# Block 0's stores of the second third on one queue, more weight sums on GpSimd, and planned gaps between transposed loads

## The chip, the cores and the metric

The kernel runs on one core of one Trainium2 chip. The metric is the device time of one execution in microseconds (us), the median of several runs. The engines are called PE (TensorE, matmuls), DVE (VectorE), ACT (ScalarE), POOL (GpSimd) and SP (SyncE, which here only issues DMAs).

## The reference

```python
batch, m, k, h, n = 16, 512, 768, 3072, 768     # x, w1, b1, w2: float32
y = np.matmul(x, w1) + b1
y = np.maximum(y, 0)
return np.matmul(y, w2).astype(np.float32)
```

As one matrix x has 8192 rows: 8192x768 times 768x3072, bias and ReLU, times 3072x768.

## The kernel before

**Data and tiling.** Everything is computed in fp16 with fp32 sums. The 8192 rows are 8 blocks of 1024. The 3072 columns of the first matmul are three "thirds" g = 0, 1, 2. Of a third, w1 is 8 raw pieces (2 halves of k times 4 column groups h, a "strip" being one (g, h)); of a block, x is 8 raw pieces. Instead of 32 block products the kernel makes 26, each of a sum of x pieces with a sum of w1 pieces (the tables `X_SUMS` and `W1_SUMS`: 19 and 18 additions of a 128x768 tile); the results are combined by ACT and DVE on their way out of PSUM (`add_first`; the operations are "sum", "seed", which writes into a PSUM bank that a later product adds to, and "out", which writes y). Block 0 is the exception: its first two thirds are made by plain products without sums (`first_block`, `plain`, line 1040), since the sums aren't ready yet; its last third, g = 2, is the first to use them (line 1142). Then come block 1 with g = 0, 1, 2, block 2, and so on. y goes to DRAM (`yd`) and is read back for the second matmul, which is done in the same manner (`add_second`, line 1337, with `Y_SUMS` and `W2_SUMS`).

**Names.** `v` is SBUF for the weights: `v[:, g, slot]`, 24 slots for each third. Slots 8 to 23 of `v[:, 1]` are borrowed at the start: the evictions of block 0's plain products (ACT, line 1054) write y there, 16 slots in all, for g = 0 and again for g = 1. `add_store_y` (line 1021) stores a slot to `yd`. Later the w1 sums of g = 1 (line 829) are written to the same slots, and so wait for those stores. `z` holds x pieces and their sums, `s` and `yo` results on their way, `ps` is PSUM with 8 banks.

**x of later blocks.** POOL loads rows of x with a cast to fp16 (`load_x`, line 728), and SP turns them with a transposing DMA from SBUF to SBUF (`add_turn`, line 790): eight loads and eight turns for each block. The x sums of the next block (line 815) need the turns.

**Queues.** SP's and ACT's DMAs share eight semaphores, DMAHW0 to DMAHW7, which are used in turn in the program's order. A DMA first waits until the one that had its semaphore before, eight places back, has landed; that is the first DMAHW name in its row below. POOL's DMAs have eight of their own (DMASW). [...]

**The order.** A planner (`Graph`) holds every step as a task with a cost, a queue and keys that it reads and writes; `run` simulates the engines and so settles the order of instructions of every engine, which bank and which slot each step takes; `emit` then writes the program in that order. Its costs and arrival times are numbers in the code; `preset` tells it when something is there. Tables say which engine makes a sum: `W1_POOL` and `W2_POOL` list the sums (third, number) that POOL makes instead of DVE, `X1_POOL` those of block 1's x. `OUT_ACT` says which of block 0's stores ACT issues. Changing one table therefore moves other instructions too.

## Time and profile before

| what | value |
|---|---|
| median of 3 runs | 851.57 us (851.34 to 853.14) |
| the profiled execution's own time | 852.25 us |
| its span in the trace | 850.6 us |
| PE busy | 835.0 us, 98% |
| DVE / ACT / POOL busy | 702.1 / 559.9 / 272.3 us |
| granted PE clock, mean | 0.995 |

The trace counts time from the span's start; 1.65 us of the profiled execution lie outside its span. A timeline row gives start, duration, engine, line, operation and tiles; "q" after an engine's name is its sequencer, which issues DMAs; "xN" means that N like instructions were merged, and the bracket behind gives the engine's idle time before the row and what ended it. The name in the bracket is inferred: where a wait was for several things, it is the last one that the profile saw.

### The profile page before, as it was taken

The page shows a single profiled execution, that of the slowest core. Times are in us where ns is not written, and L with a number is a line of the kernel's source. Part 1 is how long each engine was busy: PE and PEld are TensorE (multiplying, and loading weights), DVE is VectorE, ACT ScalarE, POOL GpSimd, SP SyncE. Part 2 cuts the span into 40 slices and gives each one's busy share as a digit, 9 for nine tenths or more (in the row PEclk, how much of TensorE's full clock was granted, in tenths as well). Part 3 has the DMA queues.
Part 4 walks back from the last instruction along what each step waited for, and adds up shares of the span by engine and source line. Part 5 has one row for each costly group of instructions (what it writes and reads, how often), then busy time and mean ns, then how long its engine had stood idle before and what let it go on. Part 6 is the DMA issues. An engine that isn't in the chain of part 4 may idle for free. (4 is left out here: it accounts for less than half of the span.)

```text
span 850.6 us, 17854 instructions
## 1 busy us (share of the span) xinstructions
PE 835.0 (98%) x6263; PEld 614.1 (72%) x6263; DVE 702.1 (83%) x1320; ACT 559.9 (66%) x1252; POOL 272.3 (32%) x421
## 2 busy tenths in 40 slices
PE   8969999999999999999999999999999999999998
PEld 7628888888888888888876666666656665565664
DVE  5858989798998979889999988788777788777773
ACT  4528878887888778878964555565545468757421
POOL 6445874554655446444413100011000011101000
PEclk9989999999999999999999999999999999999999
DMA  9994999999999989998888989888879899988622
GB/s 218 228 224 109 232 209 237 220 213 241 214 228 215 242 215 244 228 274 275 282 257 203 273 251 284 261 220 230 240 216 275 267 226 229 242 222 272 221 76 76
DMA packets 169168, 193.32 MB, mean 227 GB/s; under 512 B 58556, under 2 KB 144644, under 8 KB 169076
## 3 DMA queue, kind: packets, MB, share of 16 engines
q1 hardware_dynamic: 112480, 119.21, 46.2%
q0 software_dynamic: 54976, 71.00, 42.9%
q10 hardware_dynamic: 1620, 1.95, 0.7%
q8 instruction: 49, 0.80, 0.4%
q14 instruction: 43, 0.35, 0.1%
HBM read 140.39 MB, written 83.95 MB: 264 GB/s over the span
## 5 line engine op out<-in xcount | busy, mean ns | idle before, releaser
L1337 PE MATMUL ps<-v,z 128*128 128x384 f16 x2496 | 407.0, 326 | 0.9 <-ACT ps L1354 0.8
L1142 PE MATMUL ps<-z,v 128*128 128x256 f16 x3432 | 375.0, 273 | 0.0
L1142 PEld LDWEIGHTS <-v 128*128 128x128 f16 x3432 | 335.6, 98 | 39.8 <-issue 0.7
L1337 PEld LDWEIGHTS <-z 128*128 128x128 f16 x2496 | 244.0, 98 | 163.2 <-issue 2.2
L1295 DVE TENSOR_TENSOR z<-z 128x768 f16<-128x768 f16 x448 | 232.9, 553 | 42.9 <-PE ps L1337 27.7
L1021 POOL DMA_DIRECT2D yd<-z x228 | 123.7, 545 | 137.5 <-ACT z L1165 65.1
L1176 DVE CUSTOM_DVE_ANT_0 z<-ps,s 128x512 f16<-128x512 f32 x220 | 145.0, 684 | 25.9 <-PE ps L1142 15.5
L1170 ACT ACTIVATE s<-ps,bt 128x256 f32<-128x256 f32 x352 | 145.1, 473 | 14.9 <-PE ps L1142 8.3
L1354 ACT ACTIVATE s<-ps 128x384 f32<-128x384 f32 (+1 forms) x151 | 73.5, 486 | 122.2 <-PE ps L1337 115.9
L1179 DVE TENSOR_TENSOR s<-ps,s 128x512 f32<-128x512 f32 x132 | 89.5, 684 | 4.9 <-PE ps L1142 4.3
L922 POOL DMA_DIRECT2D z<-in_x_dram x32 | 22.9, 736 | 193.7 <-ACT junk L926 188.5
L815 DVE TENSOR_TENSOR z<-z 128x768 f16<-128x768 f16 x147 | 80.5, 580 | 4.3 <-PE ps L1142 4.1
L926 ACT ACTIVATE junk<-z 128x768 f16<-128x768 f16 x94 | 78.8, 838 | 0.9
L1354 ACT ACTIVATE ps<-ps 128x384 f32<-128x384 f32 x80 | 38.0, 475 | 61.6 <-PE ps L1337 60.9
L1358 DVE TENSOR_TENSOR s<-ps,s 128x384 f32<-128x384 f32 x107 | 59.2, 553 | 13.0 <-PE ps L1337 12.6
L1170 ACT ACTIVATE ps<-ps,bt 128x256 f32<-128x256 f32 x88 | 39.4, 448 | 26.2 <-PE ps L1142 17.0
L1170 ACT ACTIVATE z<-ps,bt 128x256 f16<-128x256 f32 x132 | 54.7, 489 | 2.3 <-PE ps L1142 2.3
L1179 DVE TENSOR_TENSOR ps<-ps,s 128x512 f32<-128x512 f32 x66 | 45.4, 696 | 10.7 <-PE ps L1142 6.2
L1040 PE MATMUL ps<-z,v 128*128 128x256 f16 (+1 forms) x264 | 44.9, 332 | 8.0 <-ACT v L1054 6.4
L1358 DVE TENSOR_TENSOR s<-s,ps 128x384 f32<-128x384 f32 x62 | 34.2, 552 | 21.6 <-PE ps L1337 21.2
L1165 ACT ACTIVATE s<-ps 128x512 f32<-128x512 f32 x66 | 39.8, 602 | 9.8 <-DVE z L1176 6.5
L1165 ACT ACTIVATE z<-ps 128x512 f16<-128x512 f32 x66 | 39.2, 594 | 10.6 <-DVE z L1176 5.0
(59 smaller groups left out, 340.2 us busy)
## 6 DMA issues: line engine op xcount, KB each, us to landing
z<-yd SPq DMA_DIRECT2D x128, 384.0 KB, 6.9
yd<-z POOLq DMA_DIRECT2D x228, 128.0 KB, 3.7
out_dram<-s SPq DMA_DIRECT2D x127, 192.0 KB, 6.2
yd<-z SPq DMA_DIRECT2D x124, 128.0 KB, 3.2
z<-in_x_dram POOLq DMA_DIRECT2D x34, 384.0 KB, 7.7
z<-in_x_dram POOLq DMA_DIRECT2D x56, 192.0 KB, 6.1
v<-w2d SPq DMA_DIRECT2D x36, 192.0 KB, 4.0
w2d<-in_w_dram POOLq DMA_DIRECT2D x24, 192.0 KB, 5.4
```

The source lines that it names most:

```text
L815: (self.nc.gpsimd if e == "POOL" else self.nc.vector).tensor_tensor(out=self.z[:, a], in0=self.z[:, c], in1=self.z[:, d], op=ALU.add if si ...
L926: self.nc.scalar.activation(out=self.junk, in_=src, func=ACTF.Square, accum_out=None if at is None else self.stat[:, at:at + 1])
L1021: {"POOL": self.nc.gpsimd, "SP": self.nc.sync, "ACT": self.nc.scalar}[e].dma_start(out=self.ydram[:, b, slot, g].rearrange("p s m -> p (s ...
L1142: nc.tensor.matmul(pairs(self.ps[:, at, :])[:, :, j], lhsT=self.v[:, g, w, k * self.QM + j * P:k * self.QM + (j + 1) * P], rhs=x.rearrange ...
L1165: nc.scalar.activation(out=out, in_=ps, scale=float(a), func=func if kind == "out" else ACTF.Copy)
L1170: nc.scalar.activation(out=pairs(out)[:, :, j], in_=pairs(ps)[:, :, j], func=func, scale=float(a), bias=self.bt[:, n, g, j:j + 1])
L1176: nc.vector._custom_dve(TENSOR_ADD_SAT, out=out, in0=ps, in1=s, s0=F_MAX, s1=0.0)
L1179: nc.vector.tensor_tensor(out=out, in0=in0, in1=in1, op=ALU.add if a == c else ALU.subtract)
L1295: self.nc.vector.tensor_tensor(out=self.y_view(a), in0=self.y_view(c), in1=self.y_view(d), op=ALU.add if sign > 0 else ALU.subtract)
L1337: nc.tensor.matmul(self.ps[:, bank[ch].at[0], 0:NH], lhsT=self.y_view(ys[SECOND_U[p]])[:, h // 2, h % 2 * P:(h % 2 + 1) * P], rhs=self.v[: ...
L1354: nc.scalar.activation(out=out, in_=ps, func=ACTF.Copy, scale=float(a))
L1358: nc.vector.tensor_tensor(out=out, in0=in0, in1=in1, op=ALU.add if a == c else ALU.subtract)
```

## The change

1. `OUT_ACT` is never true: block 0's eight stores of g = 1, h = 2 and 3, which ACT issued, are issued by SP.
2. `W1_POOL` has 17 sums instead of 12. `X1_POOL` stays as it is: five x sums of block 1.
3. `W2_POOL` has one more sum, (0, 17), and two neighbours of `T0_ORDER`, the order of the first group of products of the second matmul, change places.
4. The planner is told, by eight presets read by block 1's turns alone, that turn s may be planned from 44 + 0.5 s on. No instruction and no wait comes of these presets; they only shape the plan.

```diff
-W1_POOL = ((0, 14), (0, 18), (0, 20), (1, 8), (1, 10), (1, 13), (1, 16), (1, 20), (1, 23), (1, 24), (1, 25), (2, 14))
+W1_POOL = ((0, 9), (0, 10), (0, 11), (0, 13), (0, 21), (1, 8), (1, 9), (1, 12), (1, 14), (1, 20), (1, 21), (1, 23), (1, 24), (1, 25), (2, 12), (2, 14), (2, 19))
...
-OUT_ACT = lambda g, h, m, r: g == 1 and h > 1
+OUT_ACT = lambda g, h, m, r: False
...
-W2_POOL = ((0, 11), (0, 12), (0, 18), ...
+W2_POOL = ((0, 11), (0, 12), (0, 17), (0, 18), ...
...
+TURN_AT = 44, 0.5
-T0_ORDER = (13, 4, 17, 15, 12, 8, 2, 1, 10, 21, 18, 3, 25, 0, 19, 11, 23, 14, 16, 22, 7, 24, 6, 5, 20, 9)
+T0_ORDER = (13, 4, 17, 15, 12, 8, 2, 1, 10, 21, 18, 3, 25, 0, 19, 23, 11, 14, 16, 22, 7, 24, 6, 5, 20, 9)
...
         g.preset("b1_rows", 6.0)
+        for s in range(8):
+            g.preset(("turn", s), TURN_AT[0] + TURN_AT[1] * s)
...
-            reads=self.x_keys(a), writes=[("z", raw[s // 2 * 2 + k], s % 2) for k in range(2)])
+            reads=self.x_keys(a) + ([("turn", s)] if b == 1 else []), writes=[("z", raw[s // 2 * 2 + k], s % 2) for k in range(2)])
```

Since three lines are added, line 790 of before is 793 of the change, 815 is 818, 829 is 832, 1021 is 1024, 1054 is 1057, 1176 is 1179 and 1179 is 1182.

ACT at the end of block 0's second third, before: stores (line 1021) stand between the evictions of the plain products (line 1054), and the third of them waits for DMAHW6.

```order
L1054 ACTIVATE v<-ps,b1y 128x2x2x128 [waits DMAHW2_49,DMAHW1_49,PE_49]
L1054 ACTIVATE v<-ps,b1y 128x2x2x128 [waits PE_49]
L1021 DMA yd<-v 128x512 [waits DMAHW0_49,Activation_49]
L1021 DMA yd<-v 128x512 [waits DMAHW2_49]
L1054 ACTIVATE v<-ps,b1y 128x2x2x128 [waits DMAHW1_49,PE_49]
L1054 ACTIVATE v<-ps,b1y 128x2x2x128 [waits PE_49]
L1021 DMA yd<-v 128x512 [waits DMAHW6_49,Activation_49]
L1021 DMA yd<-v 128x512 [waits DMAHW0_49]
L1054 ACTIVATE v<-ps,b1y 128x2x2x128 [waits DMAHW4_49,DMAHW3_49,PE_49]
```

With the change no store is left there; the evictions wait for PE and for the stores that emptied their slots of g = 0.

```order
L1057 ACTIVATE v<-ps,b1y 128x2x2x128 [waits DMAHW2_49,DMAHW1_49,PE_49]
L1057 ACTIVATE v<-ps,b1y 128x2x2x128 [waits PE_49]
L1057 ACTIVATE v<-ps,b1y 128x2x2x128 [waits DMAHW1_49,DMAHW2_49,PE_49,Activation_49]
L1057 ACTIVATE v<-ps,b1y 128x2x2x128 [waits PE_49,Activation_49]
L1057 ACTIVATE v<-ps,b1y 128x2x2x128 [waits DMAHW4_49,DMAHW3_49,PE_49]
```

SP at the same place, before: the last store of `v` that SP makes, then block 1's eight turns (line 790) in one row; the second of them has DMAHW6.

```order
L1021 DMA yd<-v 128x512 [waits DMAHW4_49]
L790 DMA_TRANSPOSE z<-z 128x6x128 [waits DMAHW5_49,DMASW0_49,PE_49]
L790 DMA_TRANSPOSE z<-z 128x6x128 [waits DMAHW6_49,DMASW1_49]
L790 DMA_TRANSPOSE z<-z 128x6x128 [waits DMAHW7_49,DMASW2_49,PE_49]
L790 DMA_TRANSPOSE z<-z 128x6x128 [waits DMAHW1_49,DMASW3_49]
L790 DMA_TRANSPOSE z<-z 128x6x128 [waits DMAHW3_49,DMASW4_49,PE_49]
L790 DMA_TRANSPOSE z<-z 128x6x128 [waits DMAHW4_49,DMASW6_49,DMASW5_49]
L790 DMA_TRANSPOSE z<-z 128x6x128 [waits DMAHW5_49,DMASW6_49,PE_49]
L790 DMA_TRANSPOSE z<-z 128x6x128 [waits DMAHW7_49,DMASW7_49]
```

With the change four of the eight moved stores stand between the turns and four behind them.

```order
L793 DMA_TRANSPOSE z<-z 128x6x128 [waits DMAHW7_49,DMASW2_49,PE_49]
L1024 DMA yd<-v 128x512 [waits DMAHW0_49,Activation_49]
L793 DMA_TRANSPOSE z<-z 128x6x128 [waits DMAHW1_49,DMASW3_49]
L793 DMA_TRANSPOSE z<-z 128x6x128 [waits DMAHW2_49,DMASW4_49,PE_49]
L1024 DMA yd<-v 128x512 [waits DMAHW3_49,Activation_49]
L793 DMA_TRANSPOSE z<-z 128x6x128 [waits DMAHW4_49,DMASW6_49,DMASW5_49]
L1024 DMA yd<-v 128x512 [waits DMAHW5_49]
L793 DMA_TRANSPOSE z<-z 128x6x128 [waits DMAHW6_49,DMASW6_49,PE_49]
L1024 DMA yd<-v 128x512 [waits DMAHW7_49]
L793 DMA_TRANSPOSE z<-z 128x6x128 [waits DMAHW0_49,DMASW7_49]
L1024 DMA yd<-v 128x512 [waits DMAHW1_49,Activation_49]
```

POOL from the last loads of w1 (line 715) to its first store of a sum-made y, before: three w1 sums, seven loads of x, one sum, the last load of x, four sums.

```order
L715 DMA v<-in_w_dram 128x6x256 x8
L829 TENSOR_TENSOR v<-v 128x768 x3
L728 DMA z<-in_x_dram 128x768 x7
L829 TENSOR_TENSOR v<-v 128x768
L728 DMA z<-in_x_dram 128x768
L829 TENSOR_TENSOR v<-v 128x768 x4
L1021 DMA yd<-z 128x512 x2
```

With the change five sums stand ahead of the loads of x, and six in a row and one more behind the last of them.

```order
L716 DMA v<-in_w_dram 128x6x256 x8
L832 TENSOR_TENSOR v<-v 128x768 x5
L729 DMA z<-in_x_dram 128x768 x6
L832 TENSOR_TENSOR v<-v 128x768
L729 DMA z<-in_x_dram 128x768 x2
L832 TENSOR_TENSOR v<-v 128x768 x6
L1024 DMA yd<-z 128x512
L832 TENSOR_TENSOR v<-v 128x768
L1024 DMA yd<-z 128x512
```

DVE from its last 15 x sums of block 0 to the first seeds (line 1179, `ps<-ps,s`) of third g = 2, before: all its w1 sums for that third stand ahead of the first operation on its results (line 1176, shown as ISA).

```order
L815 TENSOR_TENSOR z<-z 128x768 x15
L829 TENSOR_TENSOR v<-v 128x768 x25
L1176 ISA z<-ps,s 128x512
L815 TENSOR_TENSOR z<-z 128x768
L1176 ISA z<-ps,s 128x512 x2
L1179 TENSOR_TENSOR s<-ps,s 128x512
L829 TENSOR_TENSOR v<-v 128x768 x2
L1179 TENSOR_TENSOR ps<-ps,s 128x512 x2
```

With the change 20 of them stand ahead, and five (the last of g = 2) between those operations.

```order
L818 TENSOR_TENSOR z<-z 128x768 x12
L832 TENSOR_TENSOR v<-v 128x768 x20
L1179 ISA z<-ps,s 128x512
L832 TENSOR_TENSOR v<-v 128x768 x4
L1179 ISA z<-ps,s 128x512 x2
L1182 TENSOR_TENSOR s<-ps,s 128x512
L832 TENSOR_TENSOR v<-v 128x768
L818 TENSOR_TENSOR z<-z 128x768
L1182 TENSOR_TENSOR ps<-ps,s 128x512 x2
```

## The prediction

> **What bounds the kernel now.** I read the page first, then PE's waits, then PE's timeline where the waits lie, then the engines that those waits name.

> ```profile
> span 850.6 us, 17854 instructions
> ...
> PE 835.0 (98%) x6263; PEld 614.1 (72%) x6263; DVE 702.1 (83%) x1320; ACT 559.9 (66%) x1252; POOL 272.3 (32%) x421
> ...
> PE   8969999999999999999999999999999999999998
> ...
> L1040 PE MATMUL ps<-z,v 128*128 128x256 f16 (+1 forms) x264 | 44.9, 332 | 8.0 <-ACT v L1054 6.4
> ```

> PE is busy for 98% of the span, so the change can win only where PE stands idle or runs slowly. The one hollow in its 40 slices that is not the very start is the third, from 42.5 to 63.8 us, with a 6. The plain products' group (line 1040) has 8.0 us of idle time. PE's list of waits and its timeline put that time in two places:

> ```profile
> PE ps L1040 <- ACT v L1054: 6.4, 1, 6.4
> PE ps L1040 <- DMA z<-in_x_dram: 1.5, 1, 1.5
> ...
> PE ps L1337 <- ACT ps L1354: 0.8, 1, 0.8
> ```

> ```profile
> 49.57 2.75 PE L1040 MATMUL ps<-z,v 128*128 128x512 f16 x12 [1.54 <-DMA z<-in_x_dram]
> 58.74 5.24 PE L1040 MATMUL ps<-z,v 128*128 128x512 f16 x12 [6.42 <-ACT v L1054]
> 63.81 26.37 PE L1142 MATMUL ps<-z,v 128*128 128x256 f16 x240
> ```

> Both idle stretches fall into the last products of block 0's second third. The second 12 matmuls are like the first 12 and take 5.24 us instead of 2.75. The windows tell why, by the clock in the column before the last two:

> ```profile
> 53.40:57.00 3.60, 0.00 (x0) 0.00 (x0) 1.31 (x3) 0.00 (x0) 1.12 (x1) 1.00 1.35 183
> 57.00:63.80 6.80, 5.06 (x12) 1.78 (x12) 0.00 (x0) 1.95 (x3) 2.10 (x2) 0.50 1.01 220
> 63.80:80.85 17.05, 17.05 (x158) 15.26 (x157) 13.22 (x23) 13.92 (x33) 8.41 (x10) 1.00 0.47 98
> ```

> After the long idle the granted clock is 0.50 until the first products of g = 2 begin, which costs 5.24 - 2.75 = 2.49 us more. From 63.80 on PE is busy without a gap: 26 products in 17.05 us, 0.656 each.

> What ACT does meanwhile:

> ```profile
> 46.20 2.53 ACTq L1021 DMA_DIRECT2D yd<-v  x2
> 48.83 1.26 ACT L1054 ACTIVATE v<-ps,b1y 128x512 f16<-128x512 f32 x2 [2.66 <-DMA yd<-v]
> 56.86 1.02 ACTq L1021 DMA_DIRECT2D yd<-v  x2
> 58.01 1.26 ACT L1054 ACTIVATE v<-ps,b1y 128x512 f16<-128x512 f32 x2 [7.91 <-issue]
> ```

> Its evictions, which empty the PSUM banks, stand behind its own stores. The first pair of stores holds its sequencer from 46.20 to 48.73, and the evictions begin at 48.83; of two in 1.26 us the first ends near 49.5, and PE goes on at 49.57. So I put the 1.54 to ACT too, though the row names a load of x. The second pair is issued only at 56.86; the evictions follow at 58.01, and PE goes on at 58.74. Why it is issued so late stands on SP:

> ```profile
> 46.40 15.08 SPq L790 DMA_TRANSPOSE z<-z  x8
> ```

> ```profile
> L790 SPq DMA_TRANSPOSE z<-z x3: 1362/2189/4249, 46.4 to 52.2; - x3
> ...
>   ACT v L1054: 7.9, 1
> ...
> DMA to landing us min/median/max: 5.2/8.9/9.7
> ```

> ```profile
> L790 SPq DMA_TRANSPOSE z<-z x4: 1226/1232/1307, 56.2 to 60.2; - x4
> ...
> DMA to landing us min/median/max: 2.8/3.4/4.2
> ```

> ACT's third store has DMAHW6, which the second turn had before it. The first three turns (first answer) need up to 9.7 us to land, and the answer lists ACT's line 1054 as held up 7.9 us by them. Later turns (second answer) take 1.23 us to issue and 2.8 to 4.2 to land.

> **The change, part by part.**

> *ACT's eight stores go to SP.* Nothing but evictions is left on ACT there. The evictions of 1.26 / 2 = 0.63 us are half of what 6 matmuls take (2.75 / 2 = 1.38), so ACT keeps up. I take out 1.54 + 6.42 + 2.49 = 10.45 us: the first product of g = 2 begins at 63.81 - 10.45 = 53.36. If some of the 2.49 remained (a clock that falls for another reason), the gain would be 7.96 at least.

> *The same stores on SP.* Four of the eight now stand between the turns. A store's issue on SP is

> ```profile
> L1021 SPq DMA_DIRECT2D yd<-v x24: 319/380/957, 12.7 to 44.0; - x24
> ```

> so 4 x 0.38 = 1.5 us. The last of the eight turns was issued at about 60.2; now at 61.7, and it lands 2.8 to 4.2 later, at 64.5 to 65.9. What needs it is DVE's x sum at 75.09 (below), which was 75.09 - 63.81 = 11.28 after the first product of g = 2 and would now be wanted at 53.36 + 11.28 = 64.64, plus whatever PE loses before. That is just met with the stall of the next part, missed by 1.3 at worst without it. I take nothing, and keep the miss for a rival. The other four stores stand behind the last turn; what waits for the slots that they empty are w1 sums of g = 1, wanted only a third (17.05) later. Of POOL's sums the one that needs a moved store is its sixth behind the loads, (1, 14); while it waits, POOL leaves DVE alone.

> *Five more w1 sums on POOL, fewer on DVE; DVE's last five of g = 2 now stand between operations on results.* The rows that price this are

> ```profile
> L829 DVE TENSOR_TENSOR v<-v x25: 545/552/4035, 34.5 to 54.2; 128x768 f16<-128x768 f16 x25
> L829 POOL TENSOR_TENSOR v<-v x8: 1632/1648/1952, 22.9 to 57.5; 128x768 f16<-128x768 f16 x8
> ```

> ```profile
> 34.49 3.49 DVE L829 TENSOR_TENSOR v<-v 128x768 f16<-128x768 f16 x7
> ...
> 42.12 12.60 DVE L829 TENSOR_TENSOR v<-v 128x768 f16<-128x768 f16 x15 [1.12 <-DMA v<-in_w_dram]
> 66.09 0.69 DVE L1176 CUSTOM_DVE_ANT_0 z<-ps,s 128x512 f16<-128x512 f32 x1 [11.37 <-PE ps L1142]
> ...
> 71.44 1.35 DVE L1179 TENSOR_TENSOR ps<-ps,s 128x512 f32<-128x512 f32 x2
> ...
> 73.30 0.68 DVE L1176 CUSTOM_DVE_ANT_0 z<-ps,s 128x512 f16<-128x512 f32 x1
> ...
> 75.09 0.55 DVE L815 TENSOR_TENSOR z<-z 128x768 f16<-128x768 f16 x1
> ```

> ```profile
> 46.12 3.24 POOL L829 TENSOR_TENSOR v<-v 128x768 f16<-128x768 f16 x2
> 55.88 3.23 POOL L829 TENSOR_TENSOR v<-v 128x768 f16<-128x768 f16 x2 [6.53 <-DMA yd<-v]
> 73.24 1.64 POOL L815 TENSOR_TENSOR z<-z 128x768 f16<-128x768 f16 x1 [2.46 <-PE ps L1142]
> ```

> Alone, a sum costs DVE 3.49 / 7 = 0.50 us; its slowest took 4.035, about 0.5 plus the 3.24 of the two POOL sums at 46.12. So sums of the two engines shut each other out, DVE losing. But a DVE operation on PSUM took its usual 0.68 at 73.30, wholly beside POOL's 1.64 at 73.24. [...]

> Before, DVE had finished its sums at 54.72 and waited 11.37 us for PE. That cover goes with the 10.45. The first seed (71.44) must be there when PE has made 13 products of g = 2, by the order: at 53.36 + 13 x 0.656 = 61.89. On DVE, from the end of the last x load on POOL (about 46.1, where POOL's row of sums begins), I count 11 sums at 0.50 and 5 operations on results at 0.65 up to and with that seed, and 7 POOL sums at 1.65 beside them. If nothing overlaps: 46.1 + 5.5 + 3.3 + 11.5 = 66.4, a stall of 4.5. If the operations on results run beside POOL: 63.1, a stall of 1.2. If POOL's (1, 14) and the one behind it come late enough, they fall out (3.3 less) and there is no stall. I take 1.6, near the middle value, because the row at 73.30 shows that overlap; bounds 0 and 4.5. What is late next is that seed, PE waiting on DVE at about 62.

> *Presets on the turns* make no instruction: 0 by themselves. *One y-side sum on POOL, two products swapped* (second matmul): PE's only idle time there is the 0.8 in the list of waits, at

> ```profile
> 440.00:460.00 20.00, 19.40 (x119) 11.60 (x119) 19.90 (x42) 7.29 (x15) 3.26 (x4) 1.00 0.79 229
> ```

> DVE is full there (19.90 of 20), POOL nearly empty; one sum moved may remove the 0.8 or add as much. I take 0, bounds ±0.8.

> *The rest of the run.* From 63.81 on PE has no gap to gain from. DVE is full over a long stretch without holding PE up:

> ```profile
> 70.00:100.00 30.00, 30.00 (x277) 26.86 (x276) 29.44 (x52) 24.28 (x58) 23.67 (x32) 1.00 0.85 173
> ```

> Five w1 sums fewer leave it 2.5 us more room; I take 0.

> **The sum.** The profiled execution took 852.25 us, 850.6 of it the span, and is 0.68 above the median. 852.25 - 10.45 + 1.6 = 843.4 for it; on the median 851.57 - 8.85 = 842.7.

> **The rivals.**

> *Case A*, the sum: 842.7, its own range 840.3 (no stall, and the 0.8 gone) to 844.5.

> *Case B*, DVE is shut out by POOL: nothing overlaps, the seed comes 4.5 late, and so long an idle stretch halves the clock again as the 6.42 did (2.49): 851.57 - 10.45 + 4.5 + 2.49 = 848.1; without the halving 845.6. The 4.035 speaks for it, the 0.68 at 73.30 against. From the rows, the idle time that halves the clock lies between 1.54 and 6.42. [...]

> *Case C*, the turns come late: behind stores, three more of them are slow like the median of the first three (2.19 instead of 1.23). The last turn then lands 2.9 later, up to 68.8, and PE waits for block 1's x sum by about 2.9: 845.6. For it: turns issued while loads of x still flow took up to 4.25. Against it: the four from 56.2 on did not.

> *Case D*, the stores were not what held the evictions: the 7.91 carries the name "issue", and the 1.54 that of a load. If the 6.42 and the slow clock stay, 851.57 - 1.54 = 850.0, no change that could be told. Against it: ACT's second pair of stores is issued at 56.86, and the evictions start right behind it.

> *Case E*, slower: the queue that held up ACT now holds up the turns. From 46.40 the last turn is SP's 12th DMA, and can go only when the fourth has landed. The fourth, if issued at 56.2 as the fourth turn was before, and both with landings of 9.7: 56.2 + 2 x 9.7 = 75.6, and the x sum wanted at 64.64 is 11.0 late, with 2.49 for the clock: 851.57 - 10.45 + 11.0 + 2.49 = 854.6. It decides where the last turn lands after 64.64 + 10.45 - 2.49 = 72.6. Against it: from 56.2 on the landings took 2.8 to 4.2.

> **How the numbers follow.** A 0.62, B 0.20, C 0.10, D 0.05, E 0.03. A measurement of this kernel can tell about 0.2%, 1.7 us. A, B and C are faster by more: 0.92; D is the same, 0.05; E slower, 0.03. The time is A's. The range begins at 840.6, a little above A's best, and reaches to 848.2, which holds B and C; D, E and the far ends of A, B and C, less than 0.2 together, lie outside.

> **What would show it.** PE's waits lose the 6.4 and the 1.5 at the plain products; ACT's timeline has evictions 1.3 apart up to about 54 and no store; line 1142 (then 1145) begins at 53 to 54, and the clock is 1.00 around it. A wait of PE of 1 to 2 us named after DVE's line 1182 near 62 shows A, over 4 with a clock of 0.50 behind it B; one at 64 to 69 that goes back to line 818 and a turn shows C. The prediction is wrong if PE's wait before 53 is still there, or if PE waits at a place after 70 where nothing waited before.

## The result, and the profile after

| kernel | median us (lowest to highest) | ratio to before (95% interval) |
|---|---|---|
| before, runs of the same job | 851.76 (851.31 to 853.14) | 1 |
| the change | 845.86 (844.26 to 847.78) | 0.9925 (0.991 to 0.994) |

The change is 5.9 us faster, in the direction and inside the range that were forecast, but 3.2 above the 842.7 taken as likeliest. The profiled execution took 844.51 us, 1.35 below the median. The changed kernel varies by 3.5 us from execution to execution, where before varied by 1.8 in this job; in the later jobs before varied by 1.8 to 5.3, so a wider spread of the change is not shown by these figures. All medians here are over every execution; one of the repeated change (2275 us) and one of the last kernel below (869 us) were slow, and the ratios leave these two out. The page of the profile:

```profile
span 842.7 us, 17860 instructions
...
PE   8999999999999999999999999999999999999998
...
L1043 PE MATMUL ps<-z,v 128*128 128x256 f16 (+1 forms) x264 | 42.1, 321 | 0.0
```

The 6 in the third slice is gone, and the plain products have no idle time left (8.0 before). PE's waits and the timelines of PE and ACT:

```profile
PE ps L1145 <- DVE ps L1182: 2.4, 1, 2.4
...
PE ps L1340 <- ACT ps L1357: 1.1, 2, 0.8
```

```profile
22.26 30.68 PE L1043 MATMUL ps<-z,v 128*128 128x256 f16 x174
52.78 8.68 PE L1145 MATMUL ps<-z,v 128*128 128x256 f16 x78
63.83 76.40 PE L1145 MATMUL ps<-z,v 128*128 128x256 f16 x692 [2.37 <-DVE ps L1182]
```

```profile
50.39 0.69 ACT L1057 ACTIVATE v<-ps,b1y 128x512 f16<-128x512 f32 x1 [0.61 <-PE ps L1043]
51.73 0.69 ACT L1057 ACTIVATE v<-ps,b1y 128x512 f16<-128x512 f32 x1 [0.66 <-PE ps L1043]
```

The plain products run through, ACT evicts every 1.3 us and waits for PE (one row, at 49.09, names a store instead, for 0.55), and g = 2 begins at 52.78 instead of 63.81. Then PE stands for 2.37 us, for a seed by DVE, at the place that the forecast named. DVE and POOL there:

```profile
55.05 0.69 DVE L1179 CUSTOM_DVE_ANT_0 z<-ps,s 128x512 f16<-128x512 f32 x1 [1.33 <-PE ps L1145]
...
58.87 0.68 DVE L1182 TENSOR_TENSOR s<-ps,s 128x512 f32<-128x512 f32 x1
59.47 1.51 DVE L832 TENSOR_TENSOR v<-v 128x768 f16<-128x768 f16 x1
60.90 2.26 DVE L818 TENSOR_TENSOR z<-z 128x768 f16<-128x768 f16 x1
63.09 1.28 DVE L1182 TENSOR_TENSOR ps<-ps,s 128x512 f32<-128x512 f32 x2
...
68.15 0.56 DVE L818 TENSOR_TENSOR z<-z 128x768 f16<-128x768 f16 x1 [1.39 <-DMA z<-z]
```

```profile
46.23 8.99 POOL L832 TENSOR_TENSOR v<-v 128x768 f16<-128x768 f16 x5
58.92 1.64 POOL L832 TENSOR_TENSOR v<-v 128x768 f16<-128x768 f16 x1 [3.71 <-ACT ps L1168]
...
61.09 1.65 POOL L832 TENSOR_TENSOR v<-v 128x768 f16<-128x768 f16 x1
```

The seed at 63.09 stands behind two DVE sums of 1.51 and 2.26 us, where a sum alone took 0.50 in before (3.49 / 7 at 34.49); both overlap a POOL sum, (1, 14) at 58.92 and (1, 20) at 61.09. 1.51 + 2.26 - 2 x 0.5 = 2.8, about PE's whole wait. A smaller loss follows: DVE's x sum at 68.15 waited 1.39 for a turned load, the eighth turn:

```profile
L793 SPq DMA_TRANSPOSE z<-z x2: 1251/1258/1264, 61.2 to 63.2; - x2
...
  DVE z L818: 1.4, 1
...
DMA to landing us min/median/max: 2.8/3.9/4.9
```

### The profile page after: what moved, and what is told of

It is laid out like the page before. It is cut to its first block, busy times and chain, and to the rows that moved or that the text cites. A ratio compares the mean times of both kernels' runs of the same rounds, so it can differ in the third digit from the quotient of the medians.

```text
span 842.7 us, 17860 instructions
## 1 busy us (share of the span) xinstructions
PE 832.9 (99%) x6263; PEld 613.9 (73%) x6263; DVE 702.7 (83%) x1314; ACT 560.1 (66%) x1252; POOL 282.6 (34%) x427
## 4 chain that ended last, share of the span: by engine, by line
PE 90%; DMA 0%; ACT 0%; DVE 0%; issue 0%; ACTq 0%
PE ps L1340 48%; PE ps L1145 42%; DMA z<-yd 0%; DVE z L1179 0%; ACT ps L1357 0%; ACT junk L929 0%; ACT s L1357 0%; DVE s L1182 0%; DVE s L1354 0%; PE ps L1452 0%; PE ps L1463 0%; ACTq L1357 0%
## 5 line engine op out<-in xcount | busy, mean ns | idle before, releaser
L1145 PEld LDWEIGHTS <-v 128*128 128x128 f16 x3432 | 335.8, 98 | 42.5 <-issue 3.5
L1298 DVE TENSOR_TENSOR z<-z 128x768 f16<-128x768 f16 x448 | 233.3, 553 | 43.1 <-PE ps L1340 27.2
L1179 DVE CUSTOM_DVE_ANT_0 z<-ps,s 128x512 f16<-128x512 f32 x220 | 144.7, 683 | 16.1 <-ACT ps L1173 7.9
L818 DVE TENSOR_TENSOR z<-z 128x768 f16<-128x768 f16 x147 | 85.0, 610 | 4.8 <-PE ps L1145 2.9
L925 POOL DMA_DIRECT2D z<-in_x_dram x32 | 22.9, 738 | 193.6 <-ACT junk L929 188.4
L1168 ACT ACTIVATE z<-ps 128x512 f16<-128x512 f32 x66 | 39.2, 595 | 10.7 <-PE ps L1145 5.7
L1043 PE MATMUL ps<-z,v 128*128 128x256 f16 (+1 forms) x264 | 42.1, 321 | 0.0
```

Source lines behind the costliest of these rows:

```text
L818: (self.nc.gpsimd if e == "POOL" else self.nc.vector).tensor_tensor(out=self.z[:, a], in0=self.z[:, c], in1=self.z[:, d], op=ALU.add if si ...
L1145: nc.tensor.matmul(pairs(self.ps[:, at, :])[:, :, j], lhsT=self.v[:, g, w, k * self.QM + j * P:k * self.QM + (j + 1) * P], rhs=x.rearrange ...
L1168: nc.scalar.activation(out=out, in_=ps, scale=float(a), func=func if kind == "out" else ACTF.Copy)
L1179: nc.vector._custom_dve(TENSOR_ADD_SAT, out=out, in0=ps, in1=s, s0=F_MAX, s1=0.0)
L1298: self.nc.vector.tensor_tensor(out=self.y_view(a), in0=self.y_view(c), in1=self.y_view(d), op=ALU.add if sign > 0 else ALU.subtract)
```

## The experiments

Each ran in five rounds beside the kernel before; "ratio" is to that, with its 95% interval.

| kernel | median us | ratio |
|---|---|---|
| before, only the stores to SP | 845.13 | 0.9920 (0.9899 to 0.9941) |
| the change, repeated | 845.39 | 0.9912 (0.9888 to 0.9937) |
| the change, stores back on ACT | 853.48 | 1.0020 (1.0009 to 1.0031) |
| the change, W1_POOL of before | 848.81 | 0.9954 (0.9941 to 0.9968) |
| the change, no presets | 843.77; repeated 844.54 | 0.9897 (0.9882 to 0.9912); 0.9927 (0.9914 to 0.9941) |
| the change, x sum 10 behind two seeds | 846.30 | 0.9929 (0.9908 to 0.9950) |
| the change, two POOL sums shortened | 843.40 | 0.9907 (0.9882 to 0.9933) |
| the change, (0, 9) and (1, 20) off POOL | 844.75 | 0.9911 (0.9897 to 0.9924) |
| that, turns ahead of stores | 845.16 | 0.9915 (0.9894 to 0.9936) |
| no presets, turns ahead of stores | 843.12 | 0.9888 (0.9869 to 0.9908) |
| that, (1, 12) off POOL | 845.12 | 0.9918 (0.9903 to 0.9933) |

**The stores alone.** In the kernel before:

```diff
-OUT_ACT = lambda g, h, m, r: g == 1 and h > 1
+OUT_ACT = lambda g, h, m, r: False
```

> The kernel before with ACT's eight stores given to SP, and nothing else of the change. Theory S: this alone removes PE's waits of 1.5 and 6.4 us and the slow clock, 10.5 to 10.8 us; DVE then keeps 28 sums ahead of the first seed instead of 25 of w1 with POOL's five fewer, and PE waits 0 to 3 for it: 841.5 to 845, all or more than all that the whole change brought. Rival: the other tables carry a part of the gain (POOL's five more sums spare DVE, the planned gaps keep the turns apart), so that this alone gives 846 to 850, with a longer wait for DVE near 62 or for a turn.

Measured 845.13, a ratio of 0.9920 beside the whole change's 0.9912 in the same job; the waits are in PE's timeline:

```profile
52.56 8.68 PE L1142 MATMUL ps<-z,v 128*128 128x256 f16 x78
63.08 5.40 PE L1142 MATMUL ps<-z,v 128*128 128x256 f16 x48 [1.84 <-DVE ps L1179]
69.63 5.58 PE L1142 MATMUL ps<-z,v 128*128 128x256 f16 x46 [1.15 <-DVE ps L1179]
```

One table entry carries all that the change brought, as far as these intervals can tell; the 845.13 lies 0.1 above the span that was expected. The other parts do not add up to a gain that can be told.

**The rest without the stores.** The change with the old `OUT_ACT`:

```diff
-OUT_ACT = lambda g, h, m, r: False
+OUT_ACT = lambda g, h, m, r: g == 1 and h > 1
```

> The changed kernel with the eight stores given back to ACT; all else as in the change. If the stores on ACT are what made PE wait: the waits of 1.5 and 6.4 us at the plain products come back (in sum 6 to 8) with two halved windows of the clock, and line 1145 begins near 60 to 64: 849 to 852.5. Rival: the other tables had removed the wait too (the planned gaps let an earlier turn land, so ACT's third store waits less): 845 to 847.

Measured 853.48, above the span expected and 1.6 above before. PE's timeline has both waits back, and a third, the seed's:

```profile
48.98 2.75 PE L1043 MATMUL ps<-z,v 128*128 128x512 f16 x12 [1.32 <-DMA z<-in_x_dram]
59.16 4.60 PE L1043 MATMUL ps<-z,v 128*128 128x512 f16 x12 [7.43 <-ACT v L1057]
...
73.39 1.80 PE L1145 MATMUL ps<-z,v 128*128 128x256 f16 x15 [1.11 <-DVE ps L1182]
```

So the 1.5 of before, which its row put to a load of x, was ACT's: with the stores it comes (here and before), without them it goes (in every other kernel here). It isn't the load.

**The old list of POOL's sums.**

```diff
-W1_POOL = ((0, 9), (0, 10), (0, 11), (0, 13), (0, 21), (1, 8), (1, 9), (1, 12), (1, 14), (1, 20), ...
+W1_POOL = ((0, 14), (0, 18), (0, 20), (1, 8), (1, 10), (1, 13), (1, 16), (1, 20), (1, 23), ...
```

> The changed kernel with the W1_POOL of before (12 sums on POOL instead of 17); the stores, the planned gaps and the second matmul as in the change. If the five more sums spare DVE work that PE waits for: PE's wait near 62 is 1 us or more longer than in the changed kernel, 846 to 848. If they cost DVE more than they spare it (1.65 against 0.5 each): the wait is gone or under 1, 842 to 843.5. If it hangs only on which sums happen to lie around 59 to 63: within 1 of the changed kernel, and the profile names the one or two DVE sums that stood beside a POOL sum there.

Measured 848.81, above what the first case expected. PE's wait is 4.78, two stretches of 3.41 us with a clock of 0.50 follow it (65.19 to 72.01; the first is shown), and DVE's timeline has a reason that no case named:

```profile
65.19:68.60 3.41, 2.54 (x13) 1.75 (x13) 3.20 (x6) 1.04 (x3) 1.02 (x1) 0.50 0.42 143
```

```profile
58.16 1.15 DVE L832 TENSOR_TENSOR v<-v 128x768 f16<-128x768 f16 x2 [2.60 <-DMA yd<-v]
60.45 0.78 DVE L832 TENSOR_TENSOR v<-v 128x768 f16<-128x768 f16 x1 [1.14 <-DMA yd<-v]
...
65.32 1.28 DVE L1182 TENSOR_TENSOR ps<-ps,s 128x512 f32<-128x512 f32 x2
```

DVE itself stands 2.60 and 1.14 us for the moved stores, whose slots its sums of g = 1 are to fill, and the seed comes at 65.32. In the change it is POOL's queue that stands for them:

```profile
L832 POOLq EVENT_SEMAPHORE x2: 43/5235/10427, 47.9 to 48.0; - x2
```

That wait of POOL's sequencer (line 832, after) ended at 48.0 + 10.4 = 58.4, where the first moved store landed (54.1 + 4.4), and (1, 14) followed at 58.92; DVE meanwhile went on. (The bracket of POOL's row names an operation of ACT, `ps` of line 1168, which ran from 57.89 to 58.49.) What the new list does is less to spare DVE a number of sums than to choose whose queue stands when a store is late. With the old list and no presets (the stores alone, above) DVE stood too, but 2.17 us in all and only until 55.96, early enough; with the presets, which made another plan, there were two waits, until 60.45. These two kernels differ besides only in the two tables of the second matmul.

**Without the presets.**

```diff
-        for s in range(8):
-            g.preset(("turn", s), TURN_AT[0] + TURN_AT[1] * s)
...
-            reads=self.x_keys(a) + ([("turn", s)] if b == 1 else []), ...
+            reads=self.x_keys(a), ...
```

> The changed kernel without the eight presets on the turns. If the planned gaps matter: the turns land later or in another order, x sums of block 1 (line 815) are late and PE waits for one, 1.5 or more above the changed kernel: 847 and more. If they only shape the plan: within 1 of the changed kernel (844.5 to 846.5), with the wait near 62 of 1.5 to 3.3.

Measured 843.77, below the span; run once more:

> The changed kernel without the presets on the turns, once more, as the kernel to compare with. If its 843.77 (842.97 to 843.96) was the kernel's and not that job's: 843 to 844.5, every execution without a halved window of the clock, profile with waits of about 1.0 and 1.3 us. If not: 844.5 to 846, with a longer wait near 61.

844.54, just above the upper end. Its profile's two waits are 2.0 us together, the longer 1.0 (0.99 and 1.32 in the first run), about as expected. The presets bring nothing here, and perhaps cost a microsecond: but the two intervals of this one kernel, 0.9882 to 0.9912 and 0.9914 to 0.9941, do not meet, so a tenth of a per cent or two between jobs is more than an interval tells, and versions that differ by so little are not ranked here.

**Is it the two sums? One moved, two shortened.** First the x sum moved behind the seeds (by a helper that moves a task in the finished order):

```diff
+MOVES = ((('x', 1, 10), 2),)
...
         self.g.run(begin=5.0, ahead=AHEAD)
+        for key, n in MOVES:
+            self.g.move(self.g.tag[key], n)
```

> The changed kernel with one instruction moved: DVE makes x sum 10 of block 1 behind the next two seeds instead of ahead of them. In the profile that sum took 2.26 us (0.5 when alone), shut out by POOL's sum at 61.09, and the first seed followed it. Theory S: the seed comes 2.2 earlier, PE's wait near 62 falls from 2.4 to 0.2 or less, 842 to 844 (1.5 to 2.5 below the changed kernel of the same job). Rival: the seed is late for another reason (ACT, a bank), and the time stays within 0.5 of the changed kernel; or the moved sum holds up the next DVE operations as much, and the wait of 2.4 comes back some us later.

The seed came on time (0.22 of wait at 61.0) and the rival was right: the moved sum stood longer still, and PE waited behind it. DVE, then POOL:

```profile
60.48 1.28 DVE L1190 TENSOR_TENSOR ps<-ps,s 128x512 f32<-128x512 f32 x2
61.68 3.78 DVE L826 TENSOR_TENSOR z<-z 128x768 f16<-128x768 f16 x1
65.39 0.68 DVE L1190 TENSOR_TENSOR s<-ps,s 128x512 f32<-128x512 f32 x1
```

```profile
60.68 1.65 POOL L840 TENSOR_TENSOR v<-v 128x768 f16<-128x768 f16 x1
62.27 0.56 POOL L1032 DMA_DIRECT2D yd<-z  x1
62.82 0.55 POOL L737 DMA_DIRECT2D z<-in_x_dram  x1
63.38 1.66 POOL L826 TENSOR_TENSOR z<-z 128x768 f16<-128x768 f16 x1
```

3.78 us for a sum that takes 0.5 alone: it ended 0.4 after POOL's second sum did at 65.04, and did not run in the 1.05 between the two either, while POOL issued DMAs. PE's wait became 2.65 at 64.7 with a halved stretch of the clock behind it; 846.30. Moved within reach of the same POOL work, the sum was not out of its way.

Then the cause itself made small: (1, 14) and (1, 20) are made over 256 of their 768 columns, and the rest of them is left out.

```diff
+SHORT = (1, 14), (1, 20)
...
+                k = 512 if (g, o) in SHORT else 0
...
-                    out=self.v[:, g, a], in0=self.v[:, g, b], in1=self.v[:, g, d],
+                    out=self.v[:, g, a, k:768], in0=self.v[:, g, b, k:768], in1=self.v[:, g, d, k:768],
```

> The changed kernel with two of POOL's sums, (1, 14) and (1, 20), made over 256 of their 768 columns, so that they take about 0.6 us instead of 1.64 (the rest of these sums is left out); order and waits are the same. Theory S: the two DVE sums that stood at 1.51 and 2.26 fall by about 1 us each, the seed comes 1.5 to 2.1 earlier, PE's wait near 62 falls to 0.3 to 0.9, time 1.5 to 2.1 below the changed kernel. Rival: DVE was late by its own work or by a turn; then the wait stays at 2 and more.

```profile
60.26 0.54 DVE L834 TENSOR_TENSOR v<-v 128x768 f16<-128x768 f16 x1
60.72 0.54 DVE L819 TENSOR_TENSOR z<-z 128x768 f16<-128x768 f16 x1
61.19 1.28 DVE L1184 TENSOR_TENSOR ps<-ps,s 128x512 f32<-128x512 f32 x2
```

```profile
51.75 4.18 POOL L834 TENSOR_TENSOR v<-v 128x768 f16<-128x768 f16 x3
...
56.50 0.68 POOL L834 TENSOR_TENSOR v<-v 128x256 f16<-128x256 f16 x1
```

The same two DVE sums take 0.54 each, the seed comes 1.9 us earlier (61.19), and PE's wait is 0.6. But order and waits were not the same, though that had been expected. The stored y fills columns 0 to 511 of a slot, and the shortened sums write columns 512 to 767, so they no longer wait for a store: POOL had made both by 57.2, where it had made them from 58.92 to 62.74. So this run shows that the two DVE sums take 0.54 with no POOL sum beside them, which is theory S; it does not show what short sums at the old place would do. Nor can the time be told: the median, 843.40, is 2.0 below the repeated change of the same job, but the ratios are 0.9907 and 0.9912, with intervals that overlap. The rows do not tie the loss to which sum began first: at the 1.51 POOL's sum was under way (58.92) when DVE's began (59.47), but at the 2.26 and the 3.78 DVE's sum began, by the records, ahead of the POOL sum that it stood behind (60.90 against 61.09, and 61.68 against 63.38 for the second), and lost all the same.

**Taking the sum away in earnest.** (0, 9) and (1, 20) go back to DVE, in a version that leaves nothing out:

```diff
-W1_POOL = ((0, 9), (0, 10), (0, 11), (0, 13), (0, 21), (1, 8), (1, 9), (1, 12), (1, 14), (1, 20), (1, 21), ...
+W1_POOL = ((0, 10), (0, 11), (0, 13), (0, 21), (1, 8), (1, 9), (1, 12), (1, 14), (1, 21), ...
```

> The changed kernel without (0, 9) and (1, 20) in W1_POOL: DVE makes these two sums, (1, 20) much later. In the changed kernel's profile DVE's x sum 10 stood 2.26 us because POOL made (1, 20) at 61.09. Theory S: that sum takes 0.5, DVE's first seed comes before 61.6, PE's wait of 2.0 to 2.4 near 62 falls to 0 to 0.6, and no window of the clock is halved after it: 841.5 to 843.0, with a narrower spread (under 1.5) than the changed kernel's. Rival: another sum is shut out in its place, or DVE, with two sums more, is late by its own work: 844 and more.

```profile
60.35 0.55 DVE L818 TENSOR_TENSOR z<-z 128x768 f16<-128x768 f16 x1
60.82 1.28 DVE L1182 TENSOR_TENSOR ps<-ps,s 128x512 f32<-128x512 f32 x2
...
68.44 0.56 DVE L818 TENSOR_TENSOR z<-z 128x768 f16<-128x768 f16 x1 [3.96 <-DMA z<-z]
```

x sum 10 takes 0.55 and the seed's wait is 0.33; the sum ahead of it takes 1.19 (59.24), with (1, 14) still POOL's. POOL has (1, 20) no more, and no wait was dropped, so this bears out theory S without the fault of the last test. But the 844.75 missed the expectation: with the seed on time, the next x sum stands 3.96 for the eighth turn, and PE 2.70. The prediction's case C, hidden until then by the wait ahead of it, is next in line. So the turns were moved ahead of the stores (fifth to eighth):

```diff
+MOVES = (((1, 4), -1), ((1, 5), -1), ((1, 6), -2), ((1, 7), -3))
```

> The kernel without (0, 9) and (1, 20) on POOL, with block 1's fifth to eighth turns moved ahead of the three stores that stood between them (SP). In the profile without that move PE waited 2.7 us at 67 for an x sum of DVE that began at 68.44, when the eighth turn, issued at 62 to 63, had landed. Theory C: the eighth turn is issued some 1.7 us earlier, away from the next block's loads, lands at 63 to 65.5, and the wait at 67 falls to 0 to 0.8; 841.5 to 843, 2 to 3 below the kernel without the move. Rival: the turns' landing is set by what else flows (loads of block 2), not by their issue; the wait stays at 2 and more, 844 to 845.5.

The eighth turn, issued at 60.3 instead of 62.8, made DVE wait 1.8 instead of 4.0 and PE 0.55 instead of 2.70:

```profile
67.52 5.80 PE L1152 MATMUL ps<-z,v 128*128 128x256 f16 x48 [0.55 <-DVE ps L1189]
73.70 17.85 PE L1152 MATMUL ps<-z,v 128*128 128x256 f16 x162 [0.38 <-ACT s L1180]
92.11 13.26 PE L1152 MATMUL ps<-z,v 128*128 128x256 f16 x120 [0.56 <-DVE z L1186]
```

Theory C held for the place, and the time missed its 841.5 to 843. Of the 2.15 gained there, small waits at 73 and 92 took a part, and the span fell by 0.8 only; the median, 845.16, did not fall. The same move without the presets, and with (1, 12) off POOL besides:

```diff
+MOVES = (((1, 3), -1), ((1, 4), -1), ((1, 5), -2), ((1, 6), -3), ((1, 7), -4))
```

> The changed kernel without the presets on the turns, with its fourth to eighth turns moved ahead of the four stores that stood between them (SP). Without that move PE waited 1.0 for the seed near 61 and 1.3 at 67.4 for the eighth turn. Theory C: the second wait goes, the first stays: 841.8 to 843.2, 0.7 to 1.5 below the kernel without the move. Rival: the landing of the eighth turn does not move, or the stores, now behind it, hold up a sum of g = 1 on POOL: within 0.5 of 843.8, or above.

> Put together: the changed kernel without the presets on the turns and without (1, 12) in W1_POOL (DVE makes it later), and with block 1's fourth to eighth turns ahead of the four stores that stood between them. By the order, POOL's last two early sums then end before DVE makes the last two sums ahead of the first seed. If the two waits found (the seed near 61, the eighth turn near 67) are all that is left of the change's loss: both under 0.7, no halved window, 841 to 842.5, some 3 below the changed kernel. Rival: a new pair of sums falls together, or DVE, with one sum more, is late later in block 1: 843 and more.

The first gave 843.12 in the median, as expected, the lowest of all; in its profiled execution (845.97) four DVE sums from 56.03 on took 5.13 us, where four took 1.95 in the change (55.66), POOL was busy for 3.09 of the 3.41 us from 57.63, PE waited 2.72 and a halved stretch of the clock followed, where the profiles without the move had 1.0. The second gave 845.12: PE waited 1.2 for DVE (line 1187, which makes the seeds), 1.5 for ACT and 0.9 for a sum of POOL; which sums met there is not shown. No version was found that beats the change beyond what jobs differ by.

**The change once more, for its spread.**

> The changed kernel once more, for its spread (844.3 to 847.8 us in six runs, where the kernel before had 851.3 to 853.1). Theory S: what varies is PE's wait for the first seed of g = 2 near 62 us (2.4 in the profile that was seen, at 844.5), since it hangs on how sums of DVE and POOL fall beside each other; a slower execution's profile has line 1145 beginning at 52.8 as before, and a longer wait there, by what its span is above 842.7. Theory T: what varies is the landing of block 1's turns, and the longer wait is that of an x sum (line 818) near 68 to 70. Theory U: neither; the extra time lies in the second matmul (line 1340) or before 50 us.

PE's wait in this profile was shorter, 2.00, and the execution longer, 845.64. None of the three theories had the reason, which the windows have. After (the profile of 844.51), then this one:

```profile
59.95:63.37 3.42, 1.51 (x14) 1.20 (x13) 3.42 (x3) 1.07 (x3) 3.40 (x5) 1.00 0.87 187
63.37:66.78 3.41, 2.95 (x28) 2.64 (x28) 3.38 (x6) 2.07 (x6) 2.46 (x3) 1.00 0.82 151
```

```profile
60.93:64.34 3.41, 1.41 (x14) 1.11 (x13) 3.41 (x4) 0.65 (x2) 3.02 (x4) 1.00 0.92 222
64.34:67.75 3.41, 3.41 (x19) 2.43 (x17) 3.15 (x6) 1.41 (x3) 2.49 (x3) 0.50 0.92 145
67.75:71.17 3.42, 3.42 (x33) 3.07 (x32) 2.02 (x4) 2.85 (x8) 1.53 (x3) 1.00 1.12 311
```

In the stretch of 3.41 us that begins just after the wait the clock is 0.50, and 19 matmuls run where 33 run in the next such stretch. I estimate the loss from the clock at 3.41 / 2 = 1.7 us. Over 843 us such a stretch makes a mean clock of 0.998 or less; three of the change's six executions show 0.998 (845.98, 846.42, 847.78), the other three 0.999 or 1.000 (844.26, 844.51, 845.74). So the halved stretch is one cause of the spread. It isn't the whole: 845.74 had none, and executions of other versions at a clock of 1.000 differ by up to 2.9 (843.88 to 846.75 for the kernel without presets). Which wait grows in those is open, since only one execution of each run left a trace.

## Why the prediction came out as it did

*The 10.45 taken out.* Right in each part, and a little small. The first product of g = 2 began 63.81 - 52.78 = 11.03 earlier; PE's plain products had already begun 0.35 earlier (8.53 against 8.88), which is the execution's and not the change's, so 10.7. The stores alone did it, and giving them back undid it. The semaphore fits as well: the second turn, issued at 47.9 in before, landed 8.9 later, at 56.8, ACT's third store was issued at 56.86, and the evictions behind it began at 58.01, after 7.91 idle. In the change the clock was 1.00 from 47 to 63.8, so all of the 2.49 came.

*The wait for the first seed, 1.6 (0 to 4.5).* Right in place and engine, short by 0.8 in this profile: 2.37. The mechanism was the one named, sums of DVE standing behind sums of POOL (1.51 and 2.26 where 0.50 each is usual), but not by the count that was priced, seven POOL sums at 1.65. At 55.05 DVE had caught up and waited 1.33 for PE, so the five POOL sums before that cost PE nothing. The whole wait came from the last two, (1, 14) and (1, 20), of which the prediction said that, late enough, they "fall out": (1, 14) waited for the moved store's landing, and both came just late enough to meet the two DVE sums ahead of the seed. That 1.6 lay near 2.37 is partly luck.

*The turns behind four stores, taken as nothing.* The step "just met with the stall of the next part" nearly held: the eighth turn landed late enough for DVE to stand 1.4 and PE about 0.3. But a store among the turns took 0.57 at the median and up to 0.75, where 0.38 was taken from stores before the turns, and the eighth turn was issued at 63.2, not 61.7. With the seed's wait removed it cost 2.7.

*A wait of 1.6 leaves the clock alone.* This is the step that failed. The bounds read from before, 1.54 without and 6.42 with a halved clock, were right; that 1.6 would leave the clock alone with something to spare was the author's choice within them, close to the lower one, and 2.00 did cost the clock in the repeated run (0.50 for 3.41 us). A 1.7 (the estimate above) with about even odds belonged into the sum of case A.

*The presets and the list of sums, 0 by themselves.* Wrong in the parts, right in the sum, and that by luck: with the old list the presets cost some 3 us (ratios 0.9954 against 0.9920, medians 848.81 and 845.13), since DVE then stood longer and later for the moved stores; the new list takes that off DVE. Together they come to nothing that can be told. *The second matmul, 0 with 0.8 either way:* its 0.8 is still there, a second wait of 0.2 to 0.3 came, and PE's lead over before of 7.8 us at its start (438.6 against 430.8) is 8.0 at the end of the span.

*The sum.* Profiled execution: 852.25 - 844.51 = 7.7, forecast 8.85. PE's lead over before, at the start of the same product, tells where it went. It was 11.03 at the first product of g = 2 (10.45 forecast). At the 14th it was 8.5, since before had that at 63.81 + 13 x 0.656 = 72.3 and the change at 63.83; so the seed's wait took 2.5 in all, 0.9 more than forecast. At the start of the second matmul it was 7.8; small waits up to 75 us, with the eighth turn's 0.3 among them, took the other 0.7. Median: 5.9; the rest is executions with a halved stretch, and others that stay open. One execution, 847.78, came near case B's price of 848.1; it left no trace, so by which mechanism stays open. B's mechanism itself, a wait near 4.5 with the clock halved behind it, was seen in the kernel with the old list (4.78). D and E did not show: without the stores the waits were gone, and the eighth turn's landing at 68.1 was far from 72.6.

## What to carry to other kernels

A DMA on the queue of an engine that also empties PSUM can hold that engine for the landing of some quite different transfer (here ACT for 7.91 us, for a turn's); look at whose landing its semaphore waits for, and put it on a queue on which nothing else stands. When such a wait goes, read the order for what stood behind it in the shadow (here first a seed behind two blocked sums, 2.37 of wait, then a turn, 2.70 once the first was gone): each fix brought the next to light, and the sum of gains was less than its parts. And where an idle stretch is near one that was seen to cost PE its clock (here 2.00 us did, 2.37 and 2.70 did not), count that cost by chance, and look at single executions' clocks before a spread is called noise.

## What the runs showed of the hardware

```profile
61.04:64.45 3.41, 0.79 (x8) 0.56 (x6) 3.41 (x8) 0.36 (x1) 1.11 (x2) 1.00 0.93 190
64.45:67.86 3.41, 3.31 (x16) 2.31 (x16) 2.98 (x6) 1.41 (x3) 1.78 (x2) 0.50 0.97 219
```

(the kernel without presets and with the turns ahead). With 1.51 (44%, after) and 1.73 (51%, the stores alone) it was not halved:

```profile
61.40:64.81 3.41, 1.73 (x16) 1.56 (x16) 3.41 (x6) 0.85 (x3) 3.05 (x5) 1.00 0.80 213
64.81:68.22 3.41, 3.41 (x34) 3.05 (x32) 1.19 (x2) 2.02 (x6) 2.42 (x4) 1.00 1.03 171
```

In these rows the border lies between 41% and 44% busy. Behind a stretch without any PE work (0.00 of 3.41) two halved ones followed, though PE was busy in the first of them: 1.65 of 3.41 us in before (56.98 to 60.39) and 2.54 with the old list (65.19 to 68.60, above). So an idle time of some 2 us could cost 1.7 more, by the estimate above, or nothing, by how it lay on the grid: 2.37 us (after) fell over two stretches and cost nothing, while 2.00 (the repeated change) fell into one and did. The 2.70 without (0, 9) and (1, 20) on POOL cost nothing either: that execution's mean clock was 1.000. PE need not have been idle throughout: in all three stretches above it worked for 0.79 us or more, and the next was halved.

A DVE sum was also kept out for 1.05 us in which POOL issued only DMAs between two sums (61.68 above, in the kernel with x sum 10 moved). It isn't the DMAs as such: with the two POOL sums shortened, the DVE sum at 60.26 took its 0.54 while POOL still issued a DMA, from 59.99 to 60.54:

```profile
59.99 0.55 POOL L730 DMA_DIRECT2D z<-in_x_dram  x1
```

Why it was kept out stays open.
